# A hybrid attention, recurrence and expert layer on one core: where the chunks of the modulation vectors are made

## The chip, the cores and the metric

The kernel runs on one core of a Trainium2 chip. The metric is the device time of one execution in microseconds (us); three runs of the kernel before took 2052.02, 2053.97 and 2054.25 us, so its time is the median, 2053.97 us. TensorE (PE in the rows) multiplies matrices, VectorE (DVE) and ScalarE (ACT) work element by element, and SyncE (SP) issues most of the transfers between HBM and the on-chip memory. Each engine takes its instructions in the order in which the program was laid out for it.

## The reference

One layer on x of 256 tokens by 2048 features, all in float32, with a conditioning vector c:

```python
mod = jax.nn.silu(c) @ ada_w[l] + ada_b[l]
sh1, sc1, gt1, sh2, sc2, gt2 = jnp.split(mod, 6, axis=-1)
h = rms_norm(x, norm_mix_g[l]) * (1 + sc1[:, None]) + sh1[:, None]
x = x + gt1[:, None] * hybrid_mixer(h, w_in[l], w_out[l], ...)
h = rms_norm(x, norm_ffn_g[l]) * (1 + sc2[:, None]) + sh2[:, None]
x = x + gt2[:, None] * peer_ffn(h, ...)
```

The mixer projects h with `w_in`, runs a block-sparse attention with 8 heads on one half of the columns and a gated linear recurrence on the other, normalizes both and projects with `w_out`. The feed-forward part picks 16 of 16384 experts for each of 8 heads and token, and sums them. `mod` is six vectors of 2048, each a product of silu(c) with a 2048 by 2048 matrix of 16 MB. They are needed at different times: sc1 and sh1 ahead of the input projection, gt1 after the output projection, sh2 and sc2 ahead of the feed-forward part, gt2 at the very end.

## The kernel before

**Stages.** The program's order is: the statistics of x; the wide input sets; attention and recurrence, interleaved; the output projection (tile `y`); the second normalization; the projection `wq` and the expert search; and then, for some three quarters of the time, two streams of 128 MB of expert weights. The change touches the stages up to the output projection, roughly the first 470 us.

**Weights.** Every weight comes as a 1 MB transfer into one of four buffers `raw` (`load`, line 186) and is cut into two sub-tiles. `split` (line 205) makes of each the pair `wh` (rounded, on ScalarE, line 206) and `wl` (the rest, on VectorE, line 207), and TensorE multiplies in three passes (lines 355 to 357), 12 matmuls for a sub-tile (`mm_sub`).

**The wide sets.** The input projection is made in four sets (`SEGS`, lines 504 to 533): two groups of columns, "f" and "a", each over two ranges of the input features. A set holds eight PSUM banks; it goes through the input features in pairs of 128 (index `i`), four sub-tiles for each pair, 56 sub-tiles in all. The sets take 8, 16, 16 and 16 sub-tiles. When the first "f" set ends, its sums go to two tiles `part0` and `part1`; the second "f" set is added to them (line 529), and the last features are added in attention by `rest` (line 535, the blocks b0 to b3 of the schedule).

**Modulation chunks.** A chunk is 128 values of one vector: one transfer of 1 MB into a buffer (`ada_load`, line 209), then one multiply-and-sum of 128 by 2048 elements on VectorE (`ada`, line 228; a short read of the accumulator belongs to it). The first two vectors, sc1 and sh1, are 32 chunks; `ada_first` (line 483) makes them in the wide sets. In front of each sub-tile it looks AL sub-tiles ahead in the list of pairs, and as long as the furthest pair seen has not got its four chunks, it makes one. Four chunks finish a pair: ScalarE applies the modulation, `split` makes `xH` and `xL`. Most of their buffers are three tiles of tag "av1"; some of the first use tag "av", which has two.

The next two vectors, gt1 and sh2 (`VSEG`), are 32 more chunks, made in the background: `bg(r)` (line 243) adds r to a counter and makes a chunk for each whole unit. Their buffers are the two tiles of tag "av" alone, at most two loads ahead. `part0` and `part1` have the same tag:

```python
own = n >= 2 * NDC or n < ADO and n % (ADAB + ADA1) < ADAB
...
t = [vp.tile([P, 2, NT, 512], F32, tag="av", bufs=ADAB, name=f"part{i}") for i in range(2)]
```

sc2 is made on TensorE in the gaps (tile `adp`), gt2 in the feed-forward part.

**Attention.** `PROG` (line 54) is a schedule written by hand. Its parts run one after another; in a part, the generators between bars are resumed in turn, those between commas one after another, and after each resumption `mix` (line 555) calls `bg` with the number after "@". q, k and e prepare queries, keys and the recurrence's inputs; b are the `rest` blocks; c compresses keys and g makes the gates; s are softmax scores, o attention outputs, r the recurrence (its matmuls are `rp`, line 753), l the last block of the projection (`xg`). e0 and e1 read `part0`, e2 and e3 `part1`; e0, e1 and e3 by transposes into `tp_r` (line 623).

**Output projection.** 32 sub-tiles, each followed by `bg(YR)` with YR = 0.5 (line 1038). Ahead of the first gate the chunks of gt1 are completed, at the end those of sh2.

**Order on the engines.** The program's text is not the order of issue. When the program is built, a planner places the instructions on the engines: among those that are ready it takes the one that stands first in the text, shifted where `high_priority` says so (BGP = -30 puts background chunks a little back). When something is ready it judges by its own durations. An instruction that writes a tile is ready only when the buffer's earlier tile has been released, that is, after the last access to that tile anywhere in the program. So a chunk written early in the text can be placed late, and one written late can be placed early if its load has come and VectorE seems free.

Of the kernel before, what the change touches and what calls it, by code (L numbers as in the profile page):

```python
# [18 lines left out]
NDC = D // P  # L19
# [22 lines left out]
RAWB = 4  # L42
ADAB = 2
ADA1 = 3
AL = 8
AHEAD = 2

TURN, WROOM, XTURN = 24, 1088, 8
# [2 lines left out]
SEGS = (('f', 0, 2), ('a', 0, 4), ('f', 2, 6), ('a', 4, 8))  # L51
ADO = 6
XPN = 52
PROG = 'q0 b0@.2 e0,k0,k1,p0 b1@.4 e1,b2,e2 s0|s1|r0,c0,b3 c1,g0@.2 e3 o0|o1|r1@.3 r2 s3@.25 s2 l0@.25 o2|o3|r3,l1@.3'
XL = 50
BGP = -30
YR = 0.5
EPS = 1e-6
NEG = -1e30
SCALE = HD ** -0.5  # L60
# [7 lines left out]
def kernel(  # L68
# [174 lines left out]
    def bg(r):  # L243

        bgn[1] += r
        while bgn[1] >= 1.0 and bgn[0] < NDC * len(VSEG):
            bgn[1] -= 1.0
            while ada_load():
                pass
            with tc.high_priority(offset=BGP):  # L250
                ada(mod[:, VSEG[bgn[0] // NDC], bgn[0] % NDC:bgn[0] % NDC + 1])
            bgn[0] += 1
            if bgn[0] % NDC == 0:
                ada_close(VSEG[bgn[0] // NDC - 1], 0, NDC)
# [99 lines left out]
    def mm3(o, ah, al, bh, bl, first, last):  # L354
        T.matmul(o, ah, bh, start=first, stop=False)  # L355
        T.matmul(o, ah, bl, start=False, stop=False)  # L356
        T.matmul(o, al, bh, start=False, stop=last)  # L357

    def mm_sub(pst, kcs, wh, wl, first, last, aH, aL):
        for kk, kc in enumerate(kcs):  # L360
            for tb in range(NT):
                mm3(pst[tb], aH[:, kc, tbs[tb]], aL[:, kc, tbs[tb]], wh[:, kk], wl[:, kk],
                    first and kk == 0, last and kk == len(kcs) - 1)
# [78 lines left out]
    ea, e0, eq = ExitStack(), ExitStack(), ExitStack()  # L442
# [38 lines left out]
    adn = [0]  # L481
# [22 lines left out]
    for which, i0, i1 in SEGS:  # L504
        pst = wide(f"{which}{i0}")
        for i in range(i0, i1):
            ada_first(max(4 * i + 4 - adn[0], 0))
            if i == 7:
                e0.close()
            for b in range(4):  # L510
                wh, wl = get()
                nsub += 1
                soon = max(order[:nsub + AL])
                ada_first(min(4 * soon + 4 - adn[0], 1))
                mm_sub(pst[b], (2 * i, 2 * i + 1), wh, wl, i == i0, i == i1 - 1, xH, xL)
        if not sums[which]:
            if which == "f":
                t = [vp.tile([P, 2, NT, 512], F32, tag="av", bufs=ADAB, name=f"part{i}") for i in range(2)]
                sums["f"] = [[t[b // 2][:, b % 2, tb] for tb in range(NT)] for b in range(4)]
            else:  # L520
                t = sqp.tile([P, 4, NT, 512], F32, name="sums")
                sums["a"] = [[t[:, b, tb] for tb in range(NT)] for b in range(4)]
        for b in (0, 1, 2, 3) if i1 < 8 else (3, 0, 1, 2):
            for tb in range(NT):
                r = sums[which][b][tb]
                if i0 == 0:
                    A.copy(r, pst[b][tb])
                else:
                    V.tensor_tensor(r, pst[b][tb], r, OP.add)
        if not done["a"]:  # L530
            nc.sync.dma_start(con[:, C_COS:C_END], consts[:, C_COS:C_END])
            nc.sync.dma_start(row, rows.partition_broadcast(P))
        done[which] = i1
# [41 lines left out]
    e1 = ExitStack()  # L575
# [398 lines left out]

    for part_ in PROG.split():
        names, _, rate = part_.partition("@")
# [22 lines left out]
    e3 = ExitStack()  # L999
# [30 lines left out]
    for j, half in YORDER:  # L1030
        if half == 0:
            yps[j] = [ps_x(f"y{j}_{tb}") for tb in range(NT)]
        for sub in range(4):
            wh, wl = get()
            k0 = half * 8 + sub * 2
            mm_sub(yps[j], (k0, k0 + 1), wh, wl, half == 0 and sub == 0, half == 1 and sub == 3, xH, xL)
            fill(AHEAD)
            bg(YR)
        if half == 1:
# [378 lines left out]
```

## Time and profile before

| | |
|---|---|
| three runs | 2052.02, 2053.97, 2054.25 us |
| profiled execution, its own time | 2056.6 us |
| span of its instructions | 2054.8 us, 31264 instructions |
| granted TensorE clock over the span | 0.983 of full speed |
| busy share: TensorE, VectorE, ScalarE | 96%, 71%, 49% |
| line 228 (chunks): VectorE's multiply-and-sum over "av" | 64 of 2.28 us, 145.8 us |
| line 207 (weight splits) on VectorE | 649 of 1.22 us, 788.9 us |
| chain of waits, by engine | TensorE 64%, issue 16%, VectorE 12%, DMA 4% |

Busy time is that of the instructions of an engine; issue of transfers and waiting on semaphores is not in it. "PEclk" is the clock that TensorE was granted, as a share of 2.4 GHz. In a table by stretch each engine's busy time stands with the count of its instructions. The chain of waits is the chain of work that ended last, followed back from the end. A row of a timeline gives the start, the duration, the engine, the line, the operation, and in brackets what the engine waited for.

### The profile page before, as it was taken

What the parts mean: (1) busy time and instruction counts of PE and PEld (TensorE: products, weight loads), DVE (VectorE), ACT (ScalarE), POOL (GpSimd) and SP (SyncE); (2) the same over time, 40 slices, a digit from 0 to 9 for tenths busy, and PEclk for the clock granted to TensorE, in tenths of its full rate; (3) what the DMA queues carried; (4) which work ended last, traced back from release to release, by engine and by line L of the source; (5) the groups of instructions that cost most, each with busy time, mean ns of one, the idle gap of its engine ahead of it and who ended that gap; (6) DMA issues with size and microseconds to landing.
All of it is one profiled execution on the core that took longest, in us unless ns stands there. A gap on an engine that the chain in (4) does not pass through costs nothing.

```text
span 2054.8 us, 31264 instructions
## 1 busy us (share of the span) xinstructions
PE 1979.6 (96%) x12602; PEld 1751.4 (85%) x12602; DVE 1451.0 (71%) x2149; ACT 1016.1 (49%) x1454; POOL 61.0 (3%) x95
## 2 busy tenths in 40 slices
PE   5999998998999999999999999999999999999998
PEld 4777565788999999998888789899999889999997
DVE  7888999887999666546667766665555555555566
ACT  2544676455446988645444334444444444444442
POOL 0000000000000000001000000000000000000000
PEclk8999998898999999999999999999999999999999
DMA  9898778995455666778767777776555666556663
GB/s 361 333 361 337 273 302 326 343 342 207 165 179 192 227 244 244 253 262 308 256 232 259 270 263 258 256 265 209 197 199 200 214 203 208 202 203 207 198 226 130
DMA packets 75873, 509.12 MB, mean 248 GB/s; under 512 B 8528, under 2 KB 9040, under 8 KB 20176
## 3 DMA queue, kind: packets, MB, share of 16 engines
q1 hardware_dynamic: 63792, 450.50, 60.7%
q0 software_dynamic: 11936, 56.63, 8.2%
q8 instruction: 98, 1.61, 0.3%
q14 instruction: 47, 0.39, 0.1%
HBM read 478.78 MB, written 28.31 MB: 247 GB/s over the span
## 4 chain that ended last, share of the span: by engine, by line
PE 64%; issue 16%; DVE 12%; DMA 4%; ACT 2%; POOL 1%; DVEq 0%; SPq 0%; POOLq 0%; ACTq 0%
PE d L374 8%; PE d L373 8%; PE d L372 8%; PE u L356 7%; PE u L355 7%; PE u L357 7%; DVE wl L207 3%; DVE av L228 3%; DMA raw<-in_ada_w_dram 2%; PE wq L372 2%; PE wq L373 2%; PE wq L374 2%; PE y L357 1%; PE y L355 1%; PE y L356 1%
## 5 line engine op out<-in xcount | busy, mean ns | idle before, releaser
L207 DVE TENSOR_TENSOR wl<-raw,wh 128x1024 fp32r<-128x1024 f32 x649 | 788.9, 1221 | 462.8 <-ACT wh L206 460.0
L206 ACT CAST wh<-raw 128x1024 fp32r<-128x1024 f32 x649 | 679.9, 1050 | 808.7 <-PE u L357 374.2
L372 PE MATMUL d<-xH,wh 128*128 128x256 f32 x2048 | 571.4, 279 | 0.0
L374 PE MATMUL d<-xH,wl 128*128 128x256 f32 x2048 | 568.0, 277 | 0.8 <-DVE wl L207 0.7
L373 PE MATMUL d<-xL,wh 128*128 128x256 f32 x2048 | 567.6, 277 | 0.0
L356 PE MATMUL u<-wl,ah 128*128 128x512 f32 x1024 | 400.0, 391 | 4.2 <-DVE wl L207 4.2
L355 PE MATMUL u<-wh,ah 128*128 128x512 f32 x1024 | 398.9, 390 | 0.0
L357 PE MATMUL u<-wh,al 128*128 128x512 f32 x1024 | 398.6, 389 | 0.0
L374 PEld LDWEIGHTS d<-xH,wl 128*128 128x128 f32 x2048 | 384.9, 188 | 1.3 <-DVE wl L207 1.2
L372 PEld LDWEIGHTS d<-xH,wh 128*128 128x128 f32 x2048 | 385.2, 188 | 0.7
L373 PEld LDWEIGHTS d<-xL,wh 128*128 128x128 f32 x2048 | 384.9, 188 | 0.7
L356 PEld LDWEIGHTS u<-wl,ah 128*128 128x128 f32 x1024 | 192.2, 188 | 46.4 <-DVE wl L207 7.4
L357 PEld LDWEIGHTS u<-wh,al 128*128 128x128 f32 x1024 | 192.4, 188 | 40.2
L355 PEld LDWEIGHTS u<-wh,ah 128*128 128x128 f32 x1024 | 192.2, 188 | 39.7
L228 DVE SCALAR_TENSOR_TENSOR av<-av,cb 128x2048 f32<-128x2048 f32 x64 | 145.8, 2283 | 6.2 <-DMA av<-in_ada_w_dram 6.2
L1185 DVE TENSOR_TENSOR oh<-con,idT 128x1024 f32<-128x1024 f32 x64 | 78.0, 1223 | 58.4 <-PE w L1201 58.4
L1206 ACT ACTIVATE oh<-oh,gT 128x128 f32<-128x128 f32 x256 | 83.1, 396 | 24.9 <-DVE oh L1185 24.9
L372 PE MATMUL wq<-xH,wh 128*128 128x256 f32 x256 | 73.5, 288 | 2.5 <-ACT xH L206 2.5
L373 PE MATMUL wq<-xL,wh 128*128 128x256 f32 x256 | 73.2, 286 | 0.0
L374 PE MATMUL wq<-xH,wl 128*128 128x256 f32 x256 | 73.0, 285 | 0.0
L1262 DVE TENSOR_TENSOR acc<-acc,u 128x512 f32<-128x512 f32 x112 | 71.5, 679 | 0.0
L1201 PE MATMUL w<-oh 128*128 128x128 f32 x512 | 69.8, 276 | 0.2 <-ACT stg L1193 0.2
(359 smaller groups left out, 2007.9 us busy)
## 6 DMA issues: line engine op xcount, KB each, us to landing
raw<-in_down_dram SPq DMA_DIRECT2D x128, 1024.0 KB, 5.2
raw<-in_up_dram SPq DMA_DIRECT2D x128, 1024.0 KB, 5.1
av<-in_ada_w_dram SPq DMA_DIRECT2D x64, 1024.0 KB, 7.0
raw<-in_w_a_dram SPq DMA_DIRECT2D x32, 1024.0 KB, 9.0
raw<-in_ada_p_dram SPq DMA_DIRECT2D x16, 1024.0 KB, 7.1
raw<-in_w_out_dram SPq DMA_DIRECT2D x16, 1024.0 KB, 7.9
raw<-in_wq_dram SPq DMA_DIRECT2D x16, 1024.0 KB, 5.2
wd<-stg POOLq DMA_DIRECT2D x8, 2048.0 KB, 8.0
```

The costliest lines, as they stand in the source:

```text
L206: A.copy(dst_h, src)
L207: V.tensor_tensor(dst_l, src, dst_h.bitcast(F32), OP.subtract)
L228: V.scalar_tensor_tensor(out=t, in0=t, scalar=1.0, in1=cb, op0=OP.mult, op1=OP.mult, accum_out=m)
L355: T.matmul(o, ah, bh, start=first, stop=False)
L356: T.matmul(o, ah, bl, start=False, stop=False)
L357: T.matmul(o, al, bh, start=False, stop=last)
L372: T.matmul(o, wh[:, kk, ws], bH[:, kc], start=f and i % 2 == 0, stop=False)
L373: T.matmul(o, wh[:, kk, ws], bL[:, kc], start=False, stop=False)
L374: T.matmul(o, wl[:, kk, ws], bH[:, kc], start=False, stop=e and i % 2 == 1)
L1185: V.tensor_tensor(oh, iota.unsqueeze(1).unsqueeze(1).to_broadcast([P, 4, 2, P]), idT[:, 4 * q:4 * q + 4].unsqueeze(3).to_broadcast([P, 4, ...
L1206: A.activation(ohs[p_][:, k, 0], ohs[p_][:, k, 0], AF.Copy, scale=gT[:, t:t + 1])
L1262: V.tensor_tensor(a, a, pst[tb], OP.add)
```

## The change

Three numbers change and one call is added. AL, how far ahead `ada_first` looks, goes from 8 to 14 sub-tiles. When all 32 chunks of the first two vectors have been asked for, each further sub-tile of the wide sets calls `bg` with 0.5. In the schedule, the rate of o0|o1|r1 goes from 0.3 to 0.15 and that of the last part from 0.3 to 0.2. What is computed is the same.

```diff
-AL = 8
+AL = 14
...
-PROG = 'q0 b0@.2 e0,k0,k1,p0 b1@.4 e1,b2,e2 s0|s1|r0,c0,b3 c1,g0@.2 e3 o0|o1|r1@.3 r2 s3@.25 s2 l0@.25 o2|o3|r3,l1@.3'
+PROG = 'q0 b0@.2 e0,k0,k1,p0 b1@.4 e1,b2,e2 s0|s1|r0,c0,b3 c1,g0@.2 e3 o0|o1|r1@.15 r2 s3@.25 s2 l0@.25 o2|o3|r3,l1@.2'
...
+WR = 0.5
...
                 ada_first(min(4 * soon + 4 - adn[0], 1))
                 mm_sub(pst[b], (2 * i, 2 * i + 1), wh, wl, i == i0, i == i1 - 1, xH, xL)
+                if adn[0] == 2 * NDC:
+                    bg(WR)
```

## Rows read from the trace of the kernel before

**Rows 1.** The page's first part: TensorE and its weight loads, and the rest.

```profile
PE 1979.6 (96%) x12602; PEld 1751.4 (85%) x12602; DVE 1451.0 (71%) x2149; ACT 1016.1 (49%) x1454; POOL 61.0 (3%) x95
```

**Rows 2.** Engines by stretch: length; PE, PEld, DVE, ACT, POOL busy; clock; DMA; GB/s.

```profile
64.00:112.00 48.00, 45.60 (x191) 36.16 (x190) 39.64 (x44) 21.71 (x29) 0.00 (x0) 0.96 0.87 342
112.00:160.00 48.00, 45.17 (x196) 36.20 (x195) 40.99 (x43) 23.42 (x28) 0.00 (x0) 1.00 0.92 355
160.00:206.00 46.00, 44.28 (x195) 35.97 (x194) 39.62 (x51) 21.67 (x45) 0.79 (x2) 1.00 0.83 329
...
234.00:263.00 29.00, 23.77 (x231) 16.60 (x230) 29.00 (x66) 22.90 (x72) 0.00 (x0) 1.00 0.67 238
263.00:297.00 34.00, 34.00 (x179) 20.93 (x180) 30.24 (x79) 22.88 (x43) 0.00 (x0) 0.95 0.79 316
297.00:331.00 34.00, 27.08 (x141) 19.09 (x140) 33.77 (x72) 24.07 (x60) 0.00 (x0) 0.86 0.83 323
...
376.00:466.00 90.00, 89.84 (x424) 74.05 (x423) 79.32 (x96) 43.58 (x58) 3.28 (x6) 1.00 0.91 344
```

**Rows 3.** The same stretches, line 228 alone: length; VectorE busy (two records a chunk).

```profile
234.00:263.00 29.00, 2.29 (x2) 1.00 0.67 238
263.00:297.00 34.00, 9.90 (x9) 0.95 0.79 316
297.00:331.00 34.00, 10.72 (x10) 0.86 0.83 323
331.00:360.00 29.00, 13.74 (x12) 0.91 0.89 331
```

**Rows 4.** TensorE's waits in 297 to 331 us: us in total, times, longest.

```profile
PE rp L753 <- DVE u L748: 6.5, 1, 6.5
```

**Rows 5.** The chain of waits, 300 to 331 us: first and last of four chunks.

```profile
303.05 2.21 DVE av L228 x2
...
325.19 2.21 DVE av L228 x2
```

**Rows 6.** TensorE's timeline: last transposes out of `part0` and out of `part1`.

```profile
233.47 0.60 PE L623 MATMUL tp_r<-con,part 128*128 128x128 f32 x4
...
272.84 0.66 PE L623 MATMUL tp_r<-con,part 128*128 128x128 f32 x4
```

**Rows 7.** SP's queue: the first loads of the third vector.

```profile
234.10 0.33 SPq L219 DMA_DIRECT2D av<-in_ada_w_dram  x1
...
249.04 0.33 SPq L219 DMA_DIRECT2D av<-in_ada_w_dram  x1
...
270.76 3.09 SPq L219 DMA_DIRECT2D av<-in_ada_w_dram  x2
```

**Rows 8.** What SP's queue waited for: us in total, times, longest.

```profile
SPq L219 <- PE tp_r L623: 5.7, 2, 3.3
```

**Rows 9.** The tile av, 225 to 350 us: least, median and greatest duration.

```profile
L228 DVE SCALAR_TENSOR_TENSOR av<-av,cb x14: 2279/2282/2286, 246.7 to 344.8; 128x2048 f32<-128x2048 f32 x14
...
DMA to landing us min/median/max: 4.7/5.0/7.4
```

**Rows 10.** VectorE's timeline: first two chunks, last chunk, last evacuation of y.

```profile
246.73 2.28 DVE L228 SCALAR_TENSOR_TENSOR av<-av,cb 128x2048 f32<-128x2048 f32 x1
...
268.45 2.28 DVE L228 SCALAR_TENSOR_TENSOR av<-av,cb 128x2048 f32<-128x2048 f32 x1
...
463.75 2.28 DVE L228 SCALAR_TENSOR_TENSOR av<-av,cb 128x2048 f32<-128x2048 f32 x1
...
467.19 1.28 DVE L1014 TENSOR_TENSOR yt<-y,gtr 128x512 f32<-128x512 f32 x2
```

**Rows 11.** TensorE's timeline: the last matmul of the output projection.

```profile
465.91 0.39 PE L357 MATMUL y<-wh,xL 128*128 128x512 f32 x1
```

**Rows 12.** TensorE's waits in 112 to 160 us: us in total, times, longest.

```profile
PE f L356 <- DVE wl L207: 2.7, 2, 2.5
```

## The prediction

> **What bounds the kernel now.** I read the page's first part and found TensorE busy for 96% of the span [rows 1]; as it has its own work nearly throughout, only the stretches in which it waits can give or take time. So I cut the first 484 us (all that the change touches) at the seams of the program and read engines by stretch [rows 2], then the same cuts for the modulation chunks alone (line 228) [rows 3]. Five readings matter.
>
> In the wide sets (64 to 206 us) TensorE lacks 2.4, 2.8 and 1.7 us of 48, 48 and 46: it is the bound, with VectorE at 83 to 86%. From 234 to 263 us VectorE is busy 29.00 us of 29.00 and TensorE lacks 5.2: VectorE is the bound. From 263 to 297 us TensorE is full and VectorE has 3.8 us free. From 297 to 331 us VectorE has 0.2 us free and TensorE lacks 6.9, nearly all in one wait of 6.5 us for VectorE's convolution [rows 4]. From 376 to 466 us TensorE is full again. The chain of waits runs through four chunks of 2.2 us each just ahead of that 6.5 us wait [rows 5]. So a chunk costs its length in 234 to 263 and in 297 to 331, and nothing between or after.
>
> The second thing to see is when a chunk of the third vector can start at all. Its buffers are the two tiles of tag "av", and from the end of the first wide set these hold the partial sums `part0` and `part1`, which are read last by the transposes of `e1` and `e3`. The trace shows it: those transposes run from 233.47 and 272.84 us [rows 6], the loads are issued at 234.10 us and, held in their queue, in the pair from 270.76 us [rows 7], and the waits name it: the av load waited on `tp_r` [rows 8]. So the first chunk's load already leaves the moment `part0` is free, and from there to 273 us all chunks pass through one buffer.
>
> **The change part by part.**
>
> *Where the text puts the chunks.* A step of the schedule that is resumed adds its rate; each whole unit makes a chunk. Resumptions with a rate are b0 1, b1 1, c1,g0 4, o0|o1|r1 22, s3 6, l0 4, o2|o3|r3,l1 26. Before: 0.2+0.4+0.8+6.6+1.5+1.0+7.8 = 18.3, so 18 chunks stand ahead of the output projection. After: with AL = 14 the first 32 chunks are all asked for at sub-tile 42 of 56 instead of 48, so 15 sub-tiles add 0.5 each: 7 chunks and 0.5 over; then 0.2+0.4+0.8+3.3+1.5+1.0+5.2, in all 19.9. So 19 chunks stand ahead of the projection, and by the end of l0 14 instead of 10. The number, length and load of chunks are the same; only place and priority move.
>
> *WR, the seven chunks.* They cannot run where they are written: their loads need a buffer that `part0` and `part1` hold until 234 and 273 us [rows 6 to 8]. Nothing is queued behind a blocked load, since the planner puts a load into SP's queue only when its buffer is released. What does change is priority: at 234 us seven chunks (and an eighth, of b1) are older than all the attention work, so each goes as soon as its load lands. Loads land in 4.7, 5.0 and 7.4 us (least, median, most) in this region and a chunk takes 2.28 [rows 9], so one buffer yields one per 7.3 us: starts at 239.1, 246.4, 253.7 and, at the very edge, 261.0. Before, one chunk ran in 234 to 263 (at 246.73) and the next waited until 268.45 though its load was issued at 249.04 [rows 7, 10]. So three or four instead of one: +2 or +3; I take +2, because the fourth falls on the seam. Behind each stands everything that VectorE has queued: the weight splits, the softmax maxima, the last `part` sums, and TensorE's `rest` blocks behind those. 2 x 2.29 (one chunk with its read of the accumulator, from 2.29 for one in [rows 3]) = +4.6 us; the ends are 0 (if they only fill moments in which the planner's own schedule has VectorE free) and +6.9.
>
> The Trainium skill, "DMA: Bandwidth & Descriptors", section Bandwidth, gives 6.15 us for a 1 MB transfer (issued by GpSimd). The trace's median for the same size is 5.0 us in this region [rows 9], so the row is used. By the Trainium skill's figure the starts would be 240.3, 248.7 and 257.1, three and no fourth, and the term the same +4.6 us.
>
> From 263 us on, the text has 12 chunks ahead of r2 (8 before), so the queue of due chunks does not run dry, and two buffers yield two per 7.3 us from 273 us. In 263 to 297 there is room for 3.8 us beyond the four and a fraction now there (9.90 us by [rows 3]); two more are 4.6, so +0.8 us. Its ends: 0, and +4.6 if the idle moments lie where no chunk is at hand.
>
> *The lower rates in attention.* They thin the text between 297 and 331 us, but what runs there is what is due and has not run. Before, 10 chunks were due by the end of l0 and four or so of them ran here, 10.72 us [rows 3]. After, 14 are due by that point: 3 have run by 263 and 6 or 7 more by 297, which leaves 4 or 5. So the rates take nothing out of the stretch that VectorE bounds; I take 0, with ends -4.6 (two fewer, if the second stretch swallows eight) and +4.6 (two more, if it swallows only four). From 331 to 360 us, 13.7 us of chunks [rows 3] ran behind the attention's last matmuls; fewer there gain nothing that I can see.
>
> *The output projection.* 13.7 chunks by text before, 12.1 after, all beside a full TensorE (89.84 of 90 us). The last chunk is asked for at sub-tile 25 instead of 28 of 32. Now the last one runs at 463.75 us and a weight split behind it holds the final evacuation (467.19) although the last matmul starts at 465.91 [rows 10, 11]; at 0.39 us that matmul ends at 466.30. If the chunks end earlier, those 0.9 us are free: I take -0.8, ends 0 and -2.1 (one more split of 1.2 us off the path).
>
> *AL = 14.* The first two vectors are asked for 6 sub-tiles earlier. Only three "av1" buffers feed them, and DMA is already busy 87 and 92% of the time in 64 to 160 us, so they come perhaps 3 or 4 chunks earlier by 160 us, not 6. That puts some 3.5 x 2.29 = 8.0 us more of VectorE into 112 to 160 us, where 7.0 are free [rows 2], and takes it from 160 to 206 us, where TensorE lacks only 1.7. The stall that shows in 112 to 160, 2.7 us, is a weight split held behind chunks and `part` sums [rows 12], and more chunks there do not shorten it. I take +1.0; the ends are -6.9 (every gap of the three stretches gone) and +4 (the two waits of [rows 12] once more, and the load of weights pushed back).
>
> **Sum.** +4.6 +0.8 +0 -0.8 +1.0 = +5.6 us. The profiled execution takes 2056.6 us, of which the span is 2054.8; it becomes 2062.2. It stood 2.6 us above the median of the runs, 2053.97, so I forecast 2059.6 us for the median.
>
> **The rivals.**
>
> *It is faster: the wide sets become smooth and attention lighter.* Chunks asked for early remove the late modulation in each set (up to the 6.9 us that TensorE lacks there), and a VectorE that is free of two chunks in 297 to 331 us gives back 4.6 more. It decides when TensorE's missing time in 64 to 206 us falls below 4 us. For it: VectorE is idle for 21.8 us of these 142 [rows 2]. Against it: the stalls sit at the ends of sets. A likely size is half of it all, -5 us: 2049.
>
> The Trainium skill, "Perfetto Trace Analysis", section Optimization Strategy, says that where the most-contended engine changes over time, interleaving the regimes may help; that is this rival's argument. The trace bears the first half out (VectorE's bound at 234 and 297, TensorE's before) but shows the buffers that stop the interleaving [rows 6 to 8].
>
> *No effect, or the change does not do what it says.* The seven chunks wait for their buffers, the extra ones in 234 to 263 us drop into places where VectorE's work was not on the path, and every one run early is one less in 297 to 331. For it: the chunk at 246.73 already ran far ahead of its place in the text (g0, whose gates come after 270). Sum: 0 to +2, 2055.
>
> *Worse: attention takes the whole pile.* Three more in the first stretch (6.9), two more in the third (4.6), and 1 to 2 us in the wide sets: +13, 2067. It decides if the chunk loads keep landing in 5 us; against it, the 3.8 us free in between.
>
> **How the numbers follow.** Chances: forecast 0.47, faster 0.23, no effect 0.18, the pile 0.12. The forecast's own range is +2 to +9, 2056 to 2063. The range for 8 in 10 reaches down to the middle of the faster case (half of 0.23 is left out) and up to the middle of the pile (half of 0.12), 2049.5 to 2067. About 0.2% (4.1 us, so 2049.9 to 2058.1) is what a measurement of this kernel can tell from no change. Of the forecast case about 0.31 lies above that and 0.16 within; of the faster case 0.17 below and 0.06 within; of the case without effect 0.12 within and 0.03 on either side; the pile lies above. Faster 0.20, within 0.34, slower 0.46.
>
> **What would show it.** Right: the first av load of the third vector still leaves right behind the transposes of `part0`, no chunk of it runs ahead of 225 us, three or more run in the 29 us that follow, TensorE's missing time there grows from 5.2 to about 10, and 13 or more chunks are done when r3's `rp` matmuls start (before: 10). Wrong: a chunk of the third vector inside the wide sets; TensorE's missing time in the wide sets well below 6.9 us; or a wait ahead of `rp` well under 6.5 us.

## The result, and the profile after

The changed kernel takes 2072.43 us (median of 4 runs, 2071.24 to 2081.42) against 2052.99 us for the kernel before in the same comparison (4 runs): ratio 1.0107, 95% interval 1.0081 to 1.0132, so about 20 us slower. The profiled execution took 2072.63 us, its span 2070.9 us; it stands 16.0 us above before's 2056.6 us, which lay 3.6 us above its own median. The direction was forecast (slower, 0.46), the size was not: 2059.6 us, with 2067.0 us as the upper end.

To see where it went, the first 600 us are cut at matmuls that both kernels have. The numbers are starts of such matmuls (first and last, as the tile views give them), and the differences add up to the shift of the first `wq` matmul:

| stretch | before | after | difference | forecast |
|---|---|---|---|---|
| start to first a matmul | 64.1 | 63.1 | -1.0 | 0 |
| first a to last a (wide sets) | 141.9 | 147.4 | +5.5 | +1.0 |
| last a to last rp (attention) | 127.4 | 139.6 | +12.2 | +5.4 |
| last rp to first y | 33.4 | 35.8 | +2.4 | 0 |
| first y to last y (projection) | 99.1 | 98.2 | -0.9 | 0 |
| last y to first wq | 10.7 | 9.3 | -1.4 | -0.8 |
| sum | 476.6 | 493.4 | +16.8 | +5.6 |

First the page of the changed kernel, busy time of each engine; it answers to [rows 1]. TensorE has the same work (12602 matmuls), busy for 3.7 us longer, and 12.4 us more of the longer span are idle.

```profile
PE 1983.3 (96%) x12602; PEld 1753.1 (85%) x12602; DVE 1452.3 (70%) x2149; ACT 1017.6 (49%) x1455; POOL 60.9 (3%) x95
```

Engines by stretch of the changed kernel, the wide sets as in [rows 2]: length; PE, PEld, DVE, ACT, POOL busy; clock; DMA; GB/s.

```profile
64.00:112.00 48.00, 42.25 (x174) 33.27 (x174) 40.06 (x46) 21.07 (x26) 0.00 (x0) 0.96 0.92 365
112.00:160.00 48.00, 44.43 (x187) 35.66 (x187) 40.61 (x44) 21.64 (x27) 0.00 (x0) 0.96 0.93 371
160.00:206.00 46.00, 44.66 (x195) 36.03 (x194) 35.69 (x44) 19.04 (x31) 0.73 (x2) 1.00 0.74 287
```

TensorE lacks 5.7 and 3.6 us in the first two stretches, where it lacked 2.4 and 2.8. VectorE is no busier than before. What has risen is the last column: 365 and 371 GB/s instead of 342 and 355, and in the third stretch 287 instead of 329. Issues of transfers from 64 to 160 us, count, size and median us to landing, first the kernel before and then the changed one:

```profile
av<-in_ada_w_dram SPq DMA_DIRECT2D x16, 1024.0 KB, 7.6
raw<-in_w_a_dram SPq DMA_DIRECT2D x15, 1024.0 KB, 9.6
```

```profile
av<-in_ada_w_dram SPq DMA_DIRECT2D x18, 1024.0 KB, 8.0
raw<-in_w_a_dram SPq DMA_DIRECT2D x16, 1024.0 KB, 10.9
```

The median weight tile takes 10.9 us to land instead of 9.6. TensorE's waits in 64 to 112 us and, behind the dots, in 112 to 160 us, which answer to [rows 12] (us in total, times, longest):

```profile
PE a L356 <- ACT wh L207: 3.6, 2, 3.4
PE a L357 <- DVE wl L208: 2.2, 3, 1.1
...
PE f L356 <- ACT wh L207: 3.0, 1, 3.0
```

The two longest waits, 3.4 and 3.0 us, do not end when a tile lands. Each ends with a cast that ScalarE makes directly behind the modulation of a pair (line 495), and there ScalarE had stood for 10 and 11 us, waiting for the pair's last chunk on VectorE. ScalarE's timeline at both places, then the two weight loads on SP's queue, then their times to landing:

```profile
89.08 1.09 ACT L495 ACTIVATE xt<-xt,mod 128x256 f32<-128x256 f32 x2 [10.14 <-DVE mod L237]
90.08 1.03 ACT L207 CAST wh<-raw 128x1024 fp32r<-128x1024 f32 x1
...
132.90 1.09 ACT L495 ACTIVATE xt<-xt,mod 128x256 f32<-128x256 f32 x2 [11.37 <-DVE mod L237]
133.90 1.03 ACT L207 CAST wh<-raw 128x1024 fp32r<-128x1024 f32 x1
```

```profile
80.00 0.38 SPq L202 DMA_DIRECT2D raw<-in_w_a_dram  x1
...
122.71 0.35 SPq L202 DMA_DIRECT2D raw<-in_w_a_dram  x1
```

```profile
raw<-in_w_a_dram SPq DMA_DIRECT2D x1, 1024.0 KB, 8.0
...
raw<-in_w_a_dram SPq DMA_DIRECT2D x1, 1024.0 KB, 6.8
```

Tiles are cast in the order of their loads, two casts for each. So the first of these tiles landed at 88.0 us and was cast at 90.08, the second landed at 129.5 and was cast at 133.90: 2.1 and 4.4 us stood between, in which ScalarE waited for chunks. The kernel before has the same order on ScalarE (waits of 10.2 and 9.6 us for the modulation), but there TensorE still had sub-tiles to work on and lost no more than 0.3 us.

The attention of the changed kernel begins as forecast: last transposes out of `part0`, then the first load of the third vector (they answer to [rows 6, 7]), then its first chunks on VectorE ([rows 10]).

```profile
236.93 0.60 PE L626 MATMUL tp_r<-con,part 128*128 128x128 f32 x4
...
237.56 0.33 SPq L220 DMA_DIRECT2D av<-in_ada_w_dram  x1
...
244.55 2.28 DVE L229 SCALAR_TENSOR_TENSOR av<-av,cb 128x2048 f32<-128x2048 f32 x1
...
253.88 2.28 DVE L229 SCALAR_TENSOR_TENSOR av<-av,cb 128x2048 f32<-128x2048 f32 x1
...
263.04 2.28 DVE L229 SCALAR_TENSOR_TENSOR av<-av,cb 128x2048 f32<-128x2048 f32 x1
```

None of the seven chunks ran in the wide sets; one buffer then gives one chunk per 9.2 us, not per 7.3: a load lands in 4.8 us, but 7.0 pass from its issue to its chunk, since VectorE is not free at once. The next view is the tile av of the changed kernel from 225 to 350 us, which answers to [rows 9], and under it both kernels' `rp` matmuls, whose last number is the start of the last one (line 753 is before, 756 after).

```profile
L229 DVE SCALAR_TENSOR_TENSOR av<-av,cb x15: 2245/2283/2285, 244.5 to 347.2; 128x2048 f32<-128x2048 f32 x15
...
DMA to landing us min/median/max: 4.7/4.8/7.0
...
L756 PE MATMUL rp<-u,lw x32: 378/379/483, 253.3 to 350.1; 128*128 128x256 f32 x32
```

```profile
L753 PE MATMUL rp<-u,lw x32: 377/379/765, 244.4 to 333.4; 128*128 128x256 f32 x32
```

15 chunks start ahead of the last `rp` matmul; before it was 11, the eleventh at 331.29 us. (The prediction's "10 before, 13 or more after" counts to the start of r3's `rp`; this count goes one block further.) Attention by stretch in the changed kernel, cut 5 to 13 us later than in [rows 2] because it runs later, and the waits of its first stretch:

```profile
239.00:272.00 33.00, 24.70 (x226) 18.05 (x224) 31.14 (x63) 20.41 (x64) 0.00 (x0) 0.84 0.74 278
272.00:310.00 38.00, 33.11 (x165) 19.21 (x163) 33.22 (x83) 23.97 (x45) 0.00 (x0) 0.87 0.83 318
310.00:350.00 40.00, 37.06 (x165) 26.47 (x164) 39.14 (x83) 27.24 (x67) 0.00 (x0) 0.87 0.80 312
```

```profile
PE tp_q L626 <- DVE zr_q L616: 4.5, 1, 4.5
```

TensorE lacks 8.3 us in the first and 4.9 in the second, where before it was full from 263 to 297 us. The wait of 4.5 us is not a chunk's: it ends at 244.77 us, when the first half of `zr_q` is done and the first chunk has only begun. And the second compression weight is sent for at 260.56 us, where before it was 251.65; the compression matmuls start at 266.15 us, 5.6 us behind its issue. Two losses of the first stretch thus stand ahead of or beside the chunks and are not under them.

```profile
260.56 0.33 SPq L199 DMA_DIRECT2D raw<-in_cmp_w_dram  x1
...
266.15 3.70 PE L701 MATMUL cps<-raw,oT 128*32 128x128 f32 x128 [1.38 <-issue]
```

The whole attention in one row, from the last a matmul to the last `rp`, first the kernel before and then the changed one:

```profile
206.00:333.40 127.40, 114.55 (x702) 76.30 (x701) 122.35 (x311) 85.44 (x213) 0.00 (x0) 0.94 0.77 295
210.50:350.10 139.60, 122.27 (x702) 82.01 (x701) 131.22 (x320) 87.57 (x213) 0.00 (x0) 0.89 0.78 295
```

Of the 12.2 us only 4.5 are more waiting (TensorE is idle for 17.3 us instead of 12.9). The other 7.7 us are the same 702 matmuls taking longer, at a mean granted clock of 0.89 instead of 0.94. And the single wait that was the largest before, 6.5 us ahead of `rp` [rows 4], is gone; the changed kernel waits in other places.

The end of the projection is as forecast: the last chunk is at 468.24 us, the last y matmul follows 16 us later, and the last evacuations of y start right beside it instead of 1.3 us behind [rows 10, 11]. This is the -1.4 us in the table's last stretch. The -0.9 us between the first and last y matmul was not forecast.

```profile
468.24 2.29 DVE L229 SCALAR_TENSOR_TENSOR av<-av,cb 128x2048 f32<-128x2048 f32 x1
...
484.11 0.39 PE L358 MATMUL y<-wh,xL 128*128 128x512 f32 x1
...
484.04 1.28 DVE L1017 TENSOR_TENSOR yt<-y,gtr 128x512 f32<-128x512 f32 x2
```

### The profile page after: what moved, and what is told of

The parts are those of the page before. It is cut to its first block, busy times and chain, and to the rows that moved or that the text cites. A ratio compares the mean times of both kernels' runs of the same rounds, so it can differ in the third digit from the quotient of the medians.

```text
span 2070.9 us, 31266 instructions
## 1 busy us (share of the span) xinstructions
PE 1983.3 (96%) x12602; PEld 1753.1 (85%) x12602; DVE 1452.3 (70%) x2149; ACT 1017.6 (49%) x1455; POOL 60.9 (3%) x95
## 4 chain that ended last, share of the span: by engine, by line
PE 66%; issue 16%; DVE 11%; DMA 4%; ACT 2%; POOL 1%; DVEq 0%; SPq 0%; POOLq 0%; ACTq 0%
PE d L375 8%; PE d L373 8%; PE d L374 8%; PE u L357 7%; PE u L356 7%; PE u L358 7%; DVE wl L208 3%; DVE av L229 3%; DMA raw<-in_ada_w_dram 2%; PE wq L373 1%; PE wq L374 1%; PE wq L375 1%; PE y L356 1%; PE y L357 1%; PE y L358 1%
```

## The experiments

My theory ahead of them: two separate costs, AL = 14 in the wide sets and the seven chunks in the attention; the rates cost nothing. The rivals were that the rates are the cause, that AL explains all, and that only the combination costs.

**One part at a time.** Four kernels, each against the kernel before:

```diff
e1_al14    -AL = 8            +AL = 14
e2_wr      +WR = 0.5, with its bg(WR) behind the wide sub-tiles
e3_rates   -...r1@.3 ... l1@.3   +...r1@.15 ... l1@.2
e4_nowr    the changed kernel with WR = 0.0
```

> Only AL = 14 beside the kernel before: the first two vectors asked for six sub-tiles earlier, the program's text and its rates as they were. Theory (two separate costs): the wide sets lose about 5 us and nothing is given back later, so about +5 us (ratio 1.0025, between 1.001 and 1.004): the last matmul of the second wide set ends near 210.5 us instead of 206.0, and the attention behind it keeps its length, the output projection starting 4 to 6 us later than before's 366.8. Rival (the forecast as it was made): AL = 14 costs about +1, so no difference that can be told. Rival (AL explains it all): +15 or more, because everything later is only pushed.

> Only the new call behind the wide sub-tiles (WR = 0.5), with AL = 8 and the old rates: the first 32 chunks are then all asked for at sub-tile 48 of 56, so 4 chunks of the third vector are asked for in the wide sets instead of 7. Theory: the four can't run there, and come from 237 us on one after the other, each as soon as its load lands: wide sets as before (last matmul at 206 us, within 1), then +5 to +9 us by the output projection, ratio 1.0025 to 1.0045. Rival (place and priority of chunks don't matter, VectorE has the room): within 2 us of before. Rival (the seven only hurt because AL = 14 shifts the wide sets): within 2 us too, and the whole change's cost appears only with both.

> Only the lower rates in the program (.15 for .3 beside o0, o1 and r1, .2 for .3 at the end), AL = 8 and no call in the wide sets: 14.9 chunks asked for ahead of the output projection instead of 18.3, the rest in the projection. Theory: VectorE gets a few chunks fewer in 297 to 331 us, where it is the bound, and the projection has TensorE full and takes them: -5 to +1 us. Rival (the rates are what costs: chunks pushed into the projection hold the weight splits there): +5 us or more, with the projection longer than before's 99.1 us from its first to its last matmul.

> The changed kernel without the call in the wide sets (WR = 0): AL = 14 and the lower rates. Theory: the sum of the two runs with one of them, about +5 us from the wide sets and -5 to +1 from the rates, so 0 to +6, which puts +13 or more of the changed kernel's +19.4 on the seven chunks. Rival (AL explains it all): still +15 or more. Rival (the parts need each other): well off the sum of the single runs, by over 4 us.

Ratios to before: AL alone 1.0032 (1.0020 to 1.0044), WR alone 1.0079 (1.0061 to 1.0098), rates alone 1.0056 (1.0036 to 1.0075), the change without WR 1.0092 (1.0072 to 1.0112). AL came out as expected (+6.6 us), though its one profile places only +2.0 us ahead of the first `wq` (+5.2 in the wide sets, the rest taken back ahead of them and behind), and that execution was the fastest of its twelve. The rest went against the theory: WR alone costs 16 us, the rates alone 11, and the change without WR costs as much as the whole change. The single costs add up to 34 us, the whole is 20. The views say why. In the run with the rates alone 8 chunks start ahead of the last rp instead of 11, and the attention is 6.6 us shorter, as the theory said. But the projection asks for one chunk in two sub-tiles only (YR = 0.5), so 6 of the 32 run behind its last matmul (457.96 us), the last at 480.98, and the fourth vector is needed right there. Its timeline and its waits from 458 to 490 us:

```profile
480.98 2.29 DVE L228 SCALAR_TENSOR_TENSOR av<-av,cb 128x2048 f32<-128x2048 f32 x1 [0.18 <-DMA av<-in_ada_w_dram]
...
483.32 0.17 DVE L236 TENSOR_TENSOR mod<-mod,sm 128x16 f32<-128x16 f32 x1
```

```profile
PE wq L372 <- ACT xH L206: 16.1, 1, 16.1
```

So the low rates need the seven chunks, else the end is late; and the seven chunks are paid in the attention. The changed kernel has no late end (9.3 us from y to wq), the one without WR has 27.0 us there.

**Where the cost sits.** Four more, with the theory now that a chunk ahead of the last rp lengthens the attention, and two candidate causes for the wide sets:

```diff
e5_rates_y   rates alone, and   -YR = 0.5   +YR = 0.8
e6_defer     AL = 14 alone; chunks early, modulation of a pair where it was:
+                ada_mod(max(order[:nsub + 4]))
e7_av1       changed kernel, five chunks of the third vector in the av1 buffers:
-            own = n >= 2 * NDC or ...
+            own = n >= 2 * NDC + 5 or ...
e8_cut       kernel before, third vector:
-        V.scalar_tensor_tensor(out=t, in0=t, scalar=1.0, in1=cb, ...)
+        V.scalar_tensor_tensor(out=t[:, 0:64], in0=t[:, 0:64], scalar=1.0, in1=cb[:, 0:64], ...)
```

> The lower rates, AL = 8, no call in the wide sets, and the projection's own rate raised from 0.5 to 0.8 chunks a sub-tile (one per 3.9 us instead of 6.2). Theory now: a chunk that runs before the last rp matmul lengthens the attention by 2 us or more; 8 of them instead of 11 gave 7 us there, and the run with the lower rates alone lost them again because the text of the projection asks for only one chunk in two sub-tiles, so that 6 of the 32 ran behind its last matmul and the first wq matmul waited 16.1 us. With 0.8: the attention ends as in that run (last rp near 326 us), 30 or more chunks are done by the last y matmul, the wait of wq is under 6 us, and the whole is 3 to 8 us faster than before (ratio 0.996 to 0.9985). Rival (the projection is bound by the loads: two buffers and DMA at 0.91): still 4 or more chunks behind the last y matmul and +5 us or more. Rival: the projection itself becomes longer than 104 us.

> AL = 14 alone once more, but the two modulation operations and the split of each quad stay where they stood before (four sub-tiles ahead of their use), only the chunks go ahead. Tells what costs the 5 us of the wide sets. Theory 1 (traffic: with AL = 14 the chunks' loads come on top of weight loads in a stretch where DMA is already busy 0.92 to 0.93 of the time, and the raw tiles arrive late): first a matmul to last a matmul still takes about 147 us (AL = 14 alone 147.1, before 141.9) and the ratio stays near 1.003. Theory 2 (order: ScalarE's queue stands at a modulation operation that waits for its quad, and the weight casts behind it are late): back to 142 us or less, ratio 1.000.

> The changed kernel, but the first five chunks of the third vector take the three av1 buffers, which are free once the first two vectors are done, instead of the two that the partial sums hold. Nothing else is changed. Theory (the place decides): these five run between 180 and 215 us, beside a TensorE that is the bound there, 10 chunks instead of 15 lie before the last rp matmul, and the time from the last a matmul to the last rp falls from 139.6 to 124 to 130 us: 8 to 15 us faster than the changed kernel, ratio to before 1.001 to 1.006. Rival (what costs is something else in the attention, as the priority of the chunks or their loads): within 3 us of the changed kernel.

> The kernel before with the multiplication of each chunk of the third vector cut to 64 of its 2048 columns; what is left out is the rest of that vector's sums, loads and everything else stay. It measures the cover that the attention has for chunks. Theory (no cover: each of the 11 chunks before the last rp costs its length): last a matmul to last rp matmul falls from 127.4 to 100 to 108 us. Rival (TensorE is the bound in half of that stretch, so half of the chunks have cover): 113 to 118 us. Rival (my forecast's terms, cost in 234 to 263 and 297 to 331 us alone: one and four and a half chunks): 115 us.

The first is 1.0002 (0.9992 to 1.0013): no difference, a miss. The attention is 7.8 us shorter, but the projection takes 106.5 us instead of 99.1, with VectorE full from 376 to 396 us (20.00 of 20 us) and weights late in places (TensorE waited 2.8 us for `wh`).

The second is 1.0026 (1.0016 to 1.0036), first a to last a 146.3 us, no difference that can be told from AL = 14 alone. But it does not test what it was made for. In its trace the cast at the longest wait stands behind the modulation as before, and TensorE waits 3.4 us there again:

```profile
89.93 1.09 ACT L500 ACTIVATE xt<-xt,mod 128x256 f32<-128x256 f32 x2 [10.23 <-DVE mod L236]
90.92 1.03 ACT L206 CAST wh<-raw 128x1024 fp32r<-128x1024 f32 x1
```

So the rival that ScalarE's order costs the wide sets their time stays untested. The third is 1.0070 (1.0056 to 1.0084), 5 to 8 us faster than the changed kernel, where 8 to 15 were expected. Its five chunks did run at 189 to 208 us and the wide sets took 0.7 us more for them (148.1 against 147.4 us): there they are nearly free. But with 10 chunks left the attention took 131.5 us, not 124 to 130. TensorE's waits from 240 to 290 us name a transfer, the second compression weight: 4.9 us in one wait.

The fourth has 1.0034: slower as a whole, because its projection starts late (the fifth vector's rows were awaited for 10.2 us behind the attention, so that time is no measure here), but last a to last rp fell from 127.4 to 114.5 us, near the rivals' 113 to 118 and the 115 of my own terms, and not to the theory's 100 to 108. By the length about half of the 11 chunks had cover; but 24 matmuls of `adp`, which fill gaps, run here behind the stretch instead of in it, so the lengths are not wholly alike.

**Traffic or VectorE.**

```diff
e9_al8wr      changed kernel, -AL = 14 +AL = 8, -WR = 0.5 +WR = 0.8
e10_load      kernel before, third vector: the load is ada_w[n][:, 0:64]; VectorE's operation whole
e11_both      the same, and the operation 64 columns too
e12_al14load  AL = 14 alone; first two vectors' loads 64 columns; VectorE's operation whole
```

> The changed kernel with AL undone: AL = 8, the lower rates, and seven chunks of the third vector in the wide sets as before (WR = 0.8, since only nine sub-tiles are left behind the 32nd chunk). Theory (AL costs its 5 to 6 us whatever else is changed, and the seven chunks cost in the attention): first a to last a matmul 142 us instead of the changed kernel's 147.4, last a to last rp still 136 to 141 us, no wait of wq over 4 us: +12 to +15 us, ratio 1.006 to 1.0075. Rival (the pile depends on the early first vectors): +5 us or less.

> The kernel before, with the loads of the third vector's 16 chunks cut from 1 MB to 64 columns (32 KB); VectorE still multiplies and sums 2048 columns for each, of a constant row, so its work is the same and the traffic is gone; what is left out is that vector's values. Beside the run with the multiplication cut and the loads whole (last a to last rp 114.5 instead of 127.4). Theory (VectorE's time is the price of a chunk in the attention): last a to last rp stays within 4 us of 127.4, or grows, since chunks are ready sooner. Rival (the loads are the price): 118 us or less.

> The kernel before with both cut for the third vector: 64 columns loaded and 64 multiplied; left out is the rest of that vector. The floor for all that its chunks cost. Theory: last a to last rp 104 to 112 us (the run with only the multiplication cut lost up to 10.2 us in waits for loads of the fifth vector's rows around and behind the last rp, which this one has not), and the start of the output projection at 340 to 350 us. Rival (TensorE is the bound there already): 114 us again.

> AL = 14 alone, with the loads of the first two vectors' 32 chunks cut to 64 columns and VectorE's work as it was, on a constant row; their values are left out. Theory (traffic is what the wide sets lose by): first a to last a matmul at most 141 us (AL = 14 alone 147.1, before 141.9), with TensorE missing under 3 us in 64 to 160 instead of 9.3. Rival (VectorE's or ScalarE's queue is the cause): 145 us or more.

With AL undone the ratio is 1.0051 (1.0036 to 1.0066), 9.9 us above before; the forecast of 12 to 15 was a little high. The wide sets are back at 141.8 us and the attention is at 135.1, just under the 136 expected. Since here the wide sets end as early as before, the stretches of [rows 2, 3] can be read side by side:

```profile
234.00:263.00 29.00, 19.82 (x149) 13.10 (x147) 28.13 (x61) 20.14 (x60) 0.00 (x0) 0.94 0.57 206
263.00:297.00 34.00, 30.63 (x223) 20.97 (x224) 31.43 (x81) 22.02 (x47) 0.00 (x0) 0.90 0.89 340
```

Three chunks instead of one in the first: TensorE loses 3.95 us more (the forecast had 4.6). In the second it loses 3.4 us, where it lost nothing, while VectorE still has 2.6 us free (the forecast had 0.8). The waits say what these are. Chunk, then what the scores wait for, on VectorE; and the two longest waits of TensorE from 240 to 280 us:

```profile
250.55 2.28 DVE L229 SCALAR_TENSOR_TENSOR av<-av,cb 128x2048 f32<-128x2048 f32 x1
...
252.84 0.48 DVE L802 TENSOR_SCALAR pt<-sc,rq 128x256 f32<-128x256 f32 x1
...
253.31 0.48 DVE L803 SCALAR_TENSOR_TENSOR pt<-sc,rq,con 128x256 f32<-128x256 f32 x1
```

```profile
PE cps L701 <- DMA raw<-in_cmp_w_dram: 4.9, 1, 4.9
PE sc L811 <- DVE pt L803: 2.8, 2, 1.7
```

The 2.8 us end within 3 us of a chunk's end. The larger wait is for the second compression weight; it ends at 265.52 us, so about half of it lies in each stretch, and in the second it is most of the 3.4 us: no wait there stands behind a chunk. The weight's load leaves at 260.43 us here: SP's queue held it for 7.2 us until the first half of `cps` had freed a weight buffer, where before an earlier `adp` had freed one at 251.65 us. That the chunks bring about this other order is shown by the runs: the wait of 4.9 us is there with WR alone and with the av1 buffers too (in the changed kernel it is the late load above), and in none of the runs without WR; why the planner then places `adp` and `cps` so is not shown.

Without the loads of the third vector the attention takes 123.8 us, within the 4 us of 127.4 that the theory allowed; without its multiplications 114.5; without both 115.4 (104 to 112 was expected: a miss, TensorE's own work is the floor). Here too `adp` blurs the lengths: with the loads cut, 16 matmuls of it more than before run in the stretch (2.4 us), with both cut 22 fewer. The row with the loads cut, which answers to the two rows of the whole attention above:

```profile
203.90:327.70 123.80, 116.06 (x718) 75.51 (x717) 119.44 (x310) 85.72 (x214) 0.00 (x0) 0.99 0.61 221
```

TensorE is idle for 7.7 us in it, instead of 12.9 before and 5.4 with the multiplications or with both cut, and the wait of 6.5 us ahead of `rp` is gone in all three. So VectorE's time is the larger price in the attention, but the loads are not a small one: either cut takes away most of the waiting. With both cut TensorE is full there:

```profile
263.00:297.00 34.00, 34.00 (x191) 22.06 (x190) 26.33 (x94) 27.62 (x56) 0.00 (x0) 1.00 0.62 229
297.00:331.00 34.00, 33.94 (x162) 23.17 (x162) 28.43 (x87) 27.88 (x66) 0.00 (x0) 1.00 0.41 142
```

Now the wide sets. With the loads of the first two vectors cut and AL = 14 kept, first a to last a is 130.3 us, less than the kernel before. VectorE is busier than ever in 64 to 160 us (92.36 of 96 us), and TensorE does not wait:

```profile
64.00:160.00 96.00, 96.00 (x426) 79.50 (x425) 92.36 (x103) 52.89 (x67) 0.00 (x0) 1.00 0.59 200
```

This run takes away all the chunks' traffic, not only what AL = 14 adds, and the late pairs go with it: ScalarE waits for a modulation 1.5 us at most, instead of 11.4 in the changed kernel. So it shows that the wide sets lose nothing without the chunks' loads. It does not separate by which way the loads cost: by the weights that land later, or by the chunks that end later and hold ScalarE with a cast behind them.

**The other direction, and a search for something better.**

```diff
e13_al4     kernel before, -AL = 8 +AL = 4
e14_y65     rates alone, and -YR = 0.5 +YR = 0.65
e15_al4y65  both
```

> The kernel before with AL = 4 in place of 8: the first two vectors asked for four sub-tiles later. Theory (early loads take transfer time from the weights): DMA in 64 to 160 us falls below before's 0.89 and TensorE misses less than before's 5.2 us there: first a to last a 138 to 141 us (before 141.9), 1 to 4 us faster in all. Rival (8 is already late enough, and the modulation of a tile then comes late for its matmuls): a matmuls wait for xH, and 142 us or more, the same time or slower.

> The lower rates with AL = 8 and 0.65 chunks a sub-tile in the projection (0.5 left 6 chunks behind it, 0.8 made the projection 106.5 us long instead of 99.1). Theory (there is a middle at which the projection takes 17 or 18 chunks beside its matmuls): last y matmul 459 to 463 us, one to three chunks behind it, wait of wq under 6 us: 0 to 5 us faster than before, ratio 0.9975 to 1.000. Rival (each chunk taken out of the attention is paid again in the projection or behind it, since VectorE and the loads are as full there): within 2 us of before or slower.

> Both together: AL = 4, the lower rates, 0.65 in the projection. Theory: the sum of the two single runs, 2 to 8 us faster than before. Rival: no gain over the better of the two.

Ratios 1.0115 (1.0100 to 1.0131), 1.0027 (1.0014 to 1.0040) and 1.0127 (1.0111 to 1.0142): all slower. With AL = 4 there is less traffic in 64 to 160 us (0.79 of DMA), but now the matmuls wait for the modulation; the stretch, and TensorE's waits from 160 to 230 us:

```profile
64.00:160.00 96.00, 82.88 (x344) 66.47 (x342) 71.46 (x72) 41.27 (x49) 0.00 (x0) 0.94 0.79 306
```

```profile
PE f L355 <- ACT xH L206: 6.5, 1, 6.5
PE a L355 <- ACT xH L206: 5.6, 1, 5.6
```

With 0.65 chunks a sub-tile the attention is short again (119.4 us), the projection takes 102.3 us and `wq` still waits 11.2 us. No version tried that computes the same beats the kernel before.

The runs against the cuts of the first table, in us; in brackets the chunks that start between the last a and the last rp matmul:

| kernel | first a to last a | last a to last rp | first y to last y | last y to first wq | ratio |
|---|---|---|---|---|---|
| before | 141.9 | 127.4 (11) | 99.1 | 10.7 | |
| after | 147.4 | 139.6 (15) | 98.2 | 9.3 | 1.0107 |
| AL = 14 alone | 147.1 | 126.3 (11) | 99.0 | 10.6 | 1.0032 |
| WR alone | 141.9 | 138.3 (15) | 101.0 | 9.3 | 1.0079 |
| rates alone | 141.9 | 120.8 (8) | 99.7 | 27.2 | 1.0056 |
| after without WR | 147.4 | 121.4 (8) | 101.8 | 27.0 | 1.0092 |
| rates, YR 0.8 | 141.9 | 119.6 (8) | 106.5 | 14.8 | 1.0002 |
| AL = 14, deferred | 146.3 | 127.0 (11) | 99.2 | 10.6 | 1.0026 |
| after, av1 buffers | 148.1 | 131.5 (10) | 99.5 | 9.3 | 1.0070 |
| after, AL = 8 | 141.8 | 135.1 (15) | 98.9 | 9.3 | 1.0051 |
| rates, YR 0.65 | 141.8 | 119.4 (8) | 102.3 | 20.9 | 1.0027 |
| AL = 4 | 163.2 | 127.0 (11) | 98.9 | 10.7 | 1.0115 |
| AL = 4, rates, YR 0.65 | 163.7 | 121.6 (8) | 103.9 | 20.8 | 1.0127 |
| AL = 14, first loads cut | 130.3 | 127.3 (11) | 97.7 | 10.7 | 0.9975 |
| third vector, loads cut | 141.0 | 123.8 (11) | 102.0 | 9.3 | 1.0030 |
| third vector, operation cut | 141.9 | 114.5 (0 whole) | 99.6 | 9.4 | 1.0034 |
| third vector, both cut | 141.2 | 115.4 (0 whole) | 100.3 | 9.3 | 0.9969 |

The column of the attention has nearly the same value for the same count, whatever was done to get there (but for 131.5 at 10, where the compression weight was late, and 123.8 at 11 without their loads): 115 at none, 119 to 121 at 8, 126 to 127 at 11, 135 to 140 at 15. Per chunk that is some 0.6 us for the first eight (less, in truth, since the runs with none have 22 to 24 matmuls of `adp` fewer in the stretch), 2.2 for the next three and 2 to 3 for the next four. TensorE's idle time in the stretch is free of that: 5.4 us with none, 6.3 to 7.5 with 8, 11.6 to 14.0 with 11, 17.3 to 21.2 with 15 (7.7 with 11 without their loads). The step from 8 to 11 is a single wait: one of 5.9 to 7.5 us ahead of `rp` stands in every run with 11 chunks and their loads, and none over 0.9 us in any other.

## Why the prediction was wrong

**What held.** The seven chunks do not run where they are written; the first load leaves behind `part0`'s transposes; no chunk runs ahead of 225 us, three run in the first stretch of the attention, 15 (one block earlier 14) are done by the end of `rp`; the evacuation at the projection's end gives 1.4 us, for the reason that I gave and inside the ends of that term. The first attention term, +4.6 us, measured 3.95 with the wide sets unmoved, but the agreement is in part luck: about half of the wait for the compression weight lies in it, and the one chunk that was there before cost 0.8 us (23.77 us of TensorE against 24.54 with both cut), not its length. My chunks would start every 7.3 us and start every 9.2, which changed little. One of my signs of being wrong did come: the wait of 6.5 us ahead of `rp` is gone.

**The first step that failed: "AL = 14 ... I take +1.0".** It measured +5.5 us in the changed kernel and 5.2 alone: 3.7 us more of waiting (10.7 instead of 6.9) and 1.8 us by which the same 577 matmuls took longer. I counted the chunks against VectorE's free time. VectorE's chunk work in 64 to 160 us did not even grow (37 records of line 229 against 36 of line 228). What grew are two waits of TensorE, 3.4 and 3.0 us, both behind ScalarE, which stood at a modulation with a weight cast behind it; my sum had no such term. The loads have a share: without the chunks' loads both waits are gone. "The load of weights pushed back", which I had among the ends, is seen too (10.9 instead of 9.6 us to land; 364 to 370 GB/s over 64 to 160 us in every run with AL = 14 and whole loads, 349 before), but the two tiles behind the longest waits had landed 2.1 and 4.4 us ahead of their casts. What share it has in the 5.5 us is not shown. The Trainium skill, "DMA: Bandwidth & Descriptors", section Specifications, gives some 358 GB/s from HBM for one core. Here 371 were carried over 48 us and 421 over the 16 us from 96 to 112, with TensorE full; the measurement decides, and before's 355 was not the most that could flow.

**The second: "+0.8" for 263 to 297 and "I take 0" for 297 to 331 us.** From the first compression matmul (256.7 before, 266.2 after) to the last rp it is 76.7 us before and 83.9 after: +7.2. I priced a chunk by VectorE's free time in the stretch that it falls into, and the losses did not come that way. With AL undone VectorE still had 2.6 us free in the second stretch and TensorE lost 3.4, most of it to the compression weight, whose load the new order of work had delayed. In the changed kernel the wait of 6.5 us in the third stretch is gone, others have come (4.5 us for `zr_q` ahead of the first chunk, 2.9 for the scores, 2.6 for `ptt`), and more than half of the +12.2 is the same matmuls taking longer at a lower clock, for which I had no term, although [rows 2] show 0.95 and 0.86 there. Four more chunks were priced at 5.4 us; 3 us for each is what the stretch lost with all this in it. That nothing is queued behind a blocked load was wrong too: SP's queue held that weight's load for 7.2 us. The lower rates do not help in the changed kernel, as I said, because what is due and not run stays due; alone they do thin the attention (8 chunks, -6.6 us), which I had as an end (-4.6), but then the fourth vector is late, a wait that I did not name.

**The rival that came nearest** is the pile (+13, 2067 us). It was near in size for the attention (11.5 of its 13 us, measured 12.2), but not in the way: its two chunks more in the third stretch were to lengthen the wait there, and that wait is gone.

**What stays open.** By which way the chunks' loads cost the wide sets their time; why the clock is lower in the changed kernel's attention than with WR alone or with AL undone, where the same 15 chunks cost mainly waiting (21.2 and 18.9 us idle at 0.93 and 0.94); last rp to first y is 2.4 us longer in the changed kernel and in WR alone, and not with AL undone; the changed kernel stands some 10 us above the run with AL undone although AL alone costs 6.6; and of the 19.4 us between the medians 16.8 are placed ahead of `wq`.

## What to carry to other kernels

Background work has a price curve, not a price: count how many pieces run ahead of the matmul that ends a stage, and read how long TensorE is idle in the stage against the count. Here the first eight chunks cost 1 to 2 us together, the next three about 6 and the next four 4 to 8. Free time of an engine in a stretch is not yet room: a piece can delay, through the order of a queue, work that does not touch that engine at all, as the compression weight here. An operation that waits for a late producer is read together with what stands behind it on its engine; a modulation held ScalarE here, and TensorE waited for the cast behind it. Work that is taken out of one stage has to be followed to the place where its result is needed. And an experiment that moves a line in the text has moved nothing until the trace shows another order on the engine.

## What the runs showed of the hardware

Over 48 us the transfers ran at 371 GB/s (373 with AL = 14 alone), and in the changed kernel at 421 from 96 to 112 us, with TensorE full; a 1 MB load issued in these 16 us took 10 to 13 us to land, against 4.8 us for a chunk's load in the attention, where 200 to 340 GB/s flowed. After a short stall the granted clock was low for a while: in 239 to 272 us of the changed kernel, where TensorE once waited 4.5 us, its mean was 0.84, against 1.00 in 234 to 263 us before, where the longest wait was 1.5 us. It is at the lower of the two levels (0.50, 1.2 instead of 2.4 GHz) in the eight microseconds around the end of that wait and behind it:

```profile
244.00:252.00 8.00, 6.18 (x24) 3.76 (x25) 6.61 (x12) 2.78 (x12) 0.00 (x0) 0.50 0.53 197
```

So the attention's loss is for the larger part the same matmuls, for some of the time at the lower clock: 122.27 us busy instead of 114.55 for 702 of them. With AL undone and the same 15 chunks it was not so (116.19 us busy for 693 matmuls).
